# The last quarter of a gate-and-up tile waits unsplit, in a buffer of its own, while the down product runs

## The chip, the core and the metric

The kernel runs on one core of one Trainium2 chip. The metric is the device time of one execution in microseconds (us). Six things work at the same time: TensorE (PE in the profile, with PEld for its weight loads), VectorE (DVE), ScalarE (ACT), GpSimd (POOL), SyncE (SP, which here only issues DMAs) and the DMA engines. Each engine runs its own list of instructions; they wait for each other through semaphores.

## What is computed

One step of a decoder trunk of width 1024, on 512 prompt rows and 8 sample rows (520 columns in all, kept as two halves of 260): a SwiGLU feed-forward block, a mixer (a pooling mixer beside a state-space mixer), a second feed-forward block, a last norm. The change lies in the two feed-forward blocks alone:

```python
FFN_DIM = 2816

def _swiglu(x, wg, wu, wd):
    return (jax.nn.silu(x @ wg) * (x @ wu)) @ wd

h = h + 0.5 * _swiglu(_rms_norm(h, ffn1_norm[l]), ffn1_w_gate[l], ffn1_w_up[l], ffn1_w_down[l])
...
h = h + 0.5 * _swiglu(_rms_norm(h, ffn2_norm[l]), ffn2_w_gate[l], ffn2_w_up[l], ffn2_w_down[l])
```

All data are float32, and the outputs have to be exact to about that.

## The kernel before, in words

**Splitting.** To reach float32 accuracy from a faster matmul type, every weight tile is split into a high part (a ScalarE cast, line 107) and a low part (a VectorE subtraction, line 108), and each product is three matmuls (lines 117 to 119): high by high, high by the low part of the other side, low by high. Each matmul has 260 columns.

**Tiles of the feed-forward block.** The 2816 hidden rows are 22 tiles f of 128. For each f the gate and the up weights are loaded as one raw pair of two 128x1024 halves (lines 250 to 252). A scheme with seven products in place of eight (in the manner of Strassen) forms sums of their quarters (lines 258 to 260) and splits: the whole gate half ("a", line 253, used by products 1 and 2), two tiles of sums ("c" and "d", lines 261 and 262, used by 7 and 5, and by 6 and 3), and the last quarter of the up half ("b", line 263, used by product 4 alone). So `whi_9b` in the profile is the high part of the last quarter of f = 9. Each of the seven products is 12 matmuls (4 blocks j by 3) into one of the PSUM tiles A (products 1, 6, 7, 4) and BE (2, 3, 5).

**Homes.** The split parts "a" and "b" live in two tags, `whi` and `wlo`, with three buffers each of 128x1024 (lines 103 and 253, 263). I call a pair of such buffers a home; there are three. The weights of the down product use the same three homes (line 114). The tiles "c" and "d" have homes of their own (`shi`, `slo`, two each). A home is free again when the last matmul that reads it is done.

**Chunks.** The 22 tiles go in chunks of 8, 8 and 6 (`CHUNKS`). After the tiles of a chunk comes its down product (`down`, line 339): eight units d of 128 output rows, each with 48 matmuls over the chunk's 8 tiles (`part`, line 343), and then two VectorE instructions that add the unit to `h` (`done`, lines 356 and 360). Ahead of the down product, lines 320 to 322 of `rest` already load and split the first tile but one of the next chunk (hi + 1, which is f = 9 and f = 17), make its product 1, and finish tile hi. Its other products are written behind the down product. In the second block each unit d of the first two down products also carries one or two steps of the update of the sample states (line 377), with ScalarE instructions at line 814, VectorE ones at line 816 and DMAs on GpSimd's queue.

**What sets the order.** The program is written in the order above, and a scheduler orders each engine's list when the program is built: it runs a model of the time, and at every moment takes of each engine's instructions the one written first among those that the model holds ready. So a product that is written late can be taken early to fill a gap. A buffer goes to whoever asks first in that order. On the chip each list then runs as it stands.

**Raw buffers.** There are two raw pairs (line 92). The halves of a pair also receive down weights, two units to a pair (`raw_tile`, line 96). A pair is free when the last split or sum that reads it is done; SP then issues the next load.

Of the kernel before, what the change touches and what calls it, by code (L numbers as in the profile page):

```python
# [9 lines left out]
F32 = mybir.dt.float32  # L10
# [6 lines left out]
P = 128  # L17
# [16 lines left out]
CHUNKS = (8, 8, 6)  # L34
# [28 lines left out]
def tile_trunk_step(ctx: ExitStack, tc: tile.TileContext, ins: dict, outs: dict):  # L63
    nc = tc.nc
# [6 lines left out]
    wp = ctx.enter_context(tc.tile_pool(name="wp", bufs=3, side="right"))  # L71
# [19 lines left out]
    def raw_pair(name):  # L91
        return wp.tile([P, 2, 1024], F32, tag="raw", bufs=2, name=f"raw_{name}")
# [9 lines left out]
    def split(src, n, name, hp, nb, tags):  # L102
        hi, lo = (hp.tile([P, 1024], F32R, tag=t, bufs=nb, name=f"{t}_{name}")[:, :n] for t in tags)
        h, l = hi, lo
        if len(src.shape) == 3:
            h, l = (t.rearrange("p (j c) -> p j c", j=src.shape[1]) for t in (hi, lo))
        nc.scalar.copy(h, src)  # L107
        nc.vector.tensor_tensor(out=l, in0=src, in1=h.bitcast(F32), op=ALU.subtract)  # L108
        return hi, lo
# [6 lines left out]
    def mm3(ps, whi, wlo, xhi, xlo, start, stop, **kw):  # L116
        nc.tensor.matmul(ps, whi, xhi, start=start, stop=False, **kw)  # L117
        nc.tensor.matmul(ps, whi, xlo, start=False, stop=False, **kw)  # L118
        nc.tensor.matmul(ps, wlo, xhi, start=False, stop=stop, **kw)  # L119

    def ws(w, k, m=P):
        return w[:, k * m : (k + 1) * m]
# [73 lines left out]
    class Ffn:  # L196
# [4 lines left out]
        def __init__(self, nx, i, wx, gp, direct):  # L201
            self.nx, self.i, self.wx, self.gp, self.direct = nx, i, wx, gp, direct
            self.states = None
            self.w, self.A, self.BE, self.ac, self.g, self.tg, self.raw, self.banks, self.behind = ({} for _ in range(9))

        def plain_load(self, f, j=None):
# [40 lines left out]
        def load(self, f):  # L247
            i, wx, src = self.i, self.wx, ins[f"w{self.i}gu"]
            n = f"{i}_{f}"
            raw = raw_pair(n)  # L250
            nc.sync.dma_start(out=raw[:, 0], in_=src[2 * f])
            nc.sync.dma_start(out=raw[:, 1], in_=src[2 * f + 1])
            d1 = split(raw[:, 0], 1024, f"{n}a", wp, 3, ("whi", "wlo"))
            s1 = wx.tile([P, 2, 512], F32, tag="sw", bufs=2, name=f"s1_{n}")
            s2 = wx.tile([P, 2, 512], F32, tag="sw", bufs=2, name=f"s2_{n}")
            up0 = raw[:, 1, :512].unsqueeze(1).to_broadcast([P, 2, 512])
            diag = bass.AP(up0.tensor, up0.offset - 1024, [up0.ap[0], (1536, 2), up0.ap[2]])
            nc.vector.tensor_tensor(out=s1, in0=diag, in1=up0, op=ALU.add)  # L258
            nc.vector.tensor_tensor(out=s2[:, 0], in0=s1[:, 1], in1=raw[:, 0, :512], op=ALU.add)
            nc.vector.tensor_tensor(out=s2[:, 1], in0=s2[:, 0], in1=raw[:, 0, 512:], op=ALU.add)  # L260
            e1 = split(s1.rearrange("p q c -> p (q c)"), 1024, f"{n}c", wx, 2, ("shi", "slo"))
            e2 = split(s2.rearrange("p q c -> p (q c)"), 1024, f"{n}d", wx, 2, ("shi", "slo"))
            d2 = split(raw[:, 1, 512:], 512, f"{n}b", wp, 3, ("whi", "wlo"))
            self.w[f] = {1: (d1, 0), 2: (d1, 4), 7: (e1, 0), 5: (e1, 4), 6: (e2, 0), 3: (e2, 4), 4: (d2, 0)}

        def product(self, f, p):
            js = range(KD // 2)
            if f not in self.A:
                with tc.issue_after(self.behind[f]) if f in self.behind else nullcontext():
                    self.load(f)  # L270
                n = f"{self.i}_{f}"
                self.A[f] = ps[0].tile([P, 512], F32, tag="A", bufs=2, name=f"A{n}")
                self.BE[f] = ps[0].tile([P, 2, 512], F32, tag="BE", bufs=2, name=f"BE{n}")
                self.ac[f] = [self.wx.tile([P, 2, HB], F32, tag="ac", bufs=3, name=f"ac{n}_{q}") for q in range(2)]
            slot, dst, opens = {1: (0, 0, True), 2: (1, 1, True), 5: (3, 2, True), 6: (5, 0, False),
                                3: (2, 2, False), 7: (4, 0, False), 4: (6, 0, False)}[p]
            out = self.A[f] if dst == 0 else self.BE[f][:, dst - 1]
            (whi, wlo), k0 = self.w[f][p]
            xth, xtl = self.nx[:2]
            for j in js:  # L280
                mm3(out[:, :HB], ws(whi, k0 + j), ws(wlo, k0 + j), xth[:, j, slot], xtl[:, j, slot], opens and j == 0,
                    j == KD // 2 - 1, skip_group_check=True)
            a, c = self.ac[f]
            keep = {1: a[:, 0], 6: a[:, 1], 7: c[:, 0], 5: c[:, 1]}.get(p)
            if keep is not None:
                nc.scalar.copy(keep, out[:, :HB])  # L286
            if p == 7:
                nc.vector.tensor_tensor(out=c[:, 0], in0=c[:, 0], in1=c[:, 1], op=ALU.add)
# [800 lines left out]
```

## Time and profile before

| what | value |
|---|---|
| time of the kernel, median of 3 runs (lowest, highest) | 1012.86 us (1012.05, 1013.91) |
| time of the profiled execution | 1014.71 us |
| its span, first to last instruction | 1012.8 us |
| instructions | 19354 |
| mean granted TensorE clock | 0.993 |
| DVE busy | 807.1 us, 80% of the span |
| ACT busy | 526.1 us, 52% |
| POOL busy | 85.9 us, 8% |
| moved by DMA | 114.44 MB, mean 113 GB/s |

The four places that the change touches, by the time in the profiled execution at which the down product in question runs on PE: first block, first chunk (f = 9 waits) 110.6 to 161.1 us and second chunk (f = 17) 239.1 to 289.9; second block, first chunk 731.5 to 783.6 and second chunk 861.6 to 916.8.

How to read it: a row of the timeline gives start, duration, engine, line, operation, what it writes from what, and in brackets how long the engine sat idle before it and who released it. The duration of a matmul is modelled from issue to drain and overlaps with the next, so lost PE time is read from the distance of starts, not from busy shares alone. In rows by windows, each engine has its busy time and in brackets its number of instructions; PEclk is the granted clock, 1.00 at full speed.

### The profile page before, as it was taken

The page shows a single profiled execution, that of the slowest core. Times are in us where ns is not written, and L with a number is a line of the kernel's source. Part 1 is how long each engine was busy: PE and PEld are TensorE (multiplying, and loading weights), DVE is VectorE, ACT ScalarE, POOL GpSimd, SP SyncE. Part 2 cuts the span into 40 slices and gives each one's busy share as a digit, 9 for nine tenths or more (in the row PEclk, how much of TensorE's full clock was granted, in tenths as well). Part 3 has the DMA queues.
Part 4 walks back from the last instruction along what each step waited for, and adds up shares of the span by engine and source line. Part 5 has one row for each costly group of instructions (what it writes and reads, how often), then busy time and mean ns, then how long its engine had stood idle before and what let it go on. Part 6 is the DMA issues. An engine that isn't in the chain of part 4 may idle for free.

```text
span 1012.8 us, 19354 instructions
## 1 busy us (share of the span) xinstructions
PE 977.1 (96%) x7850; PEld 953.8 (94%) x7850; DVE 807.1 (80%) x1408; ACT 526.1 (52%) x877; POOL 85.9 (8%) x157
## 2 busy tenths in 40 slices
PE   7999999999999999999999999999999999999994
PEld 6999999999999999999899989899999999989994
DVE  7999556995569688788979987999847999467866
ACT  7566324664146455685855235666633666434552
POOL 0000000000000000157311000100013000120000
PEclk9999999999999999999999999999999999999997
DMA  6333222332223233363244421332345423453203
GB/s 193 109 125 126 84 84 94 117 105 97 92 84 105 86 105 111 103 200 116 90 144 125 141 84 43 122 126 87 122 137 184 135 108 111 103 188 123 94 32 84
DMA packets 44072, 114.44 MB, mean 113 GB/s; under 512 B 6408, under 2 KB 15560, under 8 KB 43984
## 3 DMA queue, kind: packets, MB, share of 16 engines
q1 hardware_dynamic: 40912, 103.78, 30.0%
q0 software_dynamic: 3072, 9.44, 3.8%
q8 instruction: 61, 1.00, 0.4%
q14 instruction: 27, 0.22, 0.1%
HBM read 105.86 MB, written 7.34 MB: 112 GB/s over the span
## 4 chain that ended last, share of the span: by engine, by line
PE 84%; DVE 8%; ACT 3%; DMA 2%; issue 1%; POOL 0%; SPq 0%; DVEq 0%; ACTq 0%
PE A L117 8%; PE A L118 7%; PE A L119 7%; PE dn L119 6%; PE dn L117 6%; PE BE L117 6%; PE BE L119 6%; PE dn L118 6%; PE BE L118 6%; PE P L230 2%; PE wo L117 2%; PE wo L118 2%; PE wo L119 2%; PE inz L117 2%; DMA raw<-in_w2gu 2%; PE inz L119 2%
## 5 line engine op out<-in xcount | busy, mean ns | idle before, releaser
L117 PE MATMUL dn<-g,whi_1d 128*128 128x260 f32 x352 | 99.5, 283 | 1.8 <-ACT whi_1d L107 1.6
L356 DVE SCALAR_TENSOR_TENSOR td<-dn,r_f 128x520 f32<-128x520 f32 x40 | 27.8, 698 | 90.8 <-PE dn L119 90.8
L118 PE MATMUL dn<-g,whi_1d 128*128 128x260 f32 x352 | 99.4, 283 | 0.0
L119 PE MATMUL dn<-g,wlo_1d 128*128 128x260 f32 x352 | 99.1, 283 | 0.0
L119 PE MATMUL dn<-g,wlo_2d 128*128 128x260 f32 x256 | 73.6, 288 | 3.7 <-DVE wlo_2d L108 3.7
L117 PE MATMUL dn<-g,whi_2d 128*128 128x260 f32 x256 | 73.1, 286 | 0.4 <-ACT whi_2d L107 0.4
L118 PE MATMUL dn<-g,whi_2d 128*128 128x260 f32 x256 | 73.0, 285 | 0.0
L117 PEld LDWEIGHTS dn<-g,whi_1d 128*128 128x128 f32 x352 | 66.2, 188 | 2.4 <-ACT whi_1d L107 2.0
L118 PEld LDWEIGHTS dn<-g,whi_1d 128*128 128x128 f32 x352 | 66.3, 188 | 0.0
L119 PEld LDWEIGHTS dn<-g,wlo_1d 128*128 128x128 f32 x352 | 66.1, 188 | 0.0
L286 ACT COPY ac<-A 128x260 f32<-128x260 f32 x123 | 45.8, 373 | 35.8 <-PE A L119 34.3
L107 ACT CAST whi_1d<-raw_1d 128x1024 fp32r<-128x1024 f32 (+1 forms) x24 | 23.4, 979 | 70.8 <-PE dn L118 62.3
L258 DVE TENSOR_TENSOR s<-raw 128x1024 f32<-128x1024 f32 x41 | 49.9, 1218 | 7.4 <-DMA raw<-in_w2gu 7.4
L119 PEld LDWEIGHTS dn<-g,wlo_2d 128*128 128x128 f32 x256 | 48.9, 191 | 4.6 <-DVE wlo_2d L108 4.6
L230 PE MATMUL P<-xg_f,raw 128*128 128x260 f32 x192 | 45.3, 393 | 5.8 <-DMA raw<-in_w1gu 5.3
L117 PEld LDWEIGHTS dn<-g,whi_2d 128*128 128x128 f32 x256 | 49.1, 192 | 0.6 <-ACT whi_2d L107 0.6
L118 PEld LDWEIGHTS dn<-g,whi_2d 128*128 128x128 f32 x256 | 49.0, 191 | 0.0
L230 PEld LDWEIGHTS P<-xg_f,raw 128*128 128x128 f32 x192 | 37.0, 196 | 11.7 <-ACT xg_f L179 5.3
L118 PE MATMUL wo<-catg,whi_wo 128*128 128x260 f32 x128 | 36.4, 285 | 1.3 <-DVE catg L946 1.3
L117 PE MATMUL wo<-catg,whi_wo 128*128 128x260 f32 x128 | 37.3, 292 | 0.3 <-DVE h L915 0.3
L117 PE MATMUL inz<-xh_mx,whi_inz 128*128 128x260 f32 x128 | 36.8, 287 | 0.0
L117 PE MATMUL inx<-xh_mx,whi_inx 128*128 128x260 f32 x128 | 36.4, 285 | 0.0
(1339 smaller groups left out, 3918.2 us busy)
## 6 DMA issues: line engine op xcount, KB each, us to landing
raw<-in_w2gu SPq DMA_DIRECT2D x44, 512.0 KB, 4.4
raw<-in_w1gu SPq DMA_DIRECT2D x42, 512.0 KB, 4.4
raw_1d<-in_w1d SPq DMA_DIRECT2D x16, 512.0 KB, 4.4
raw_2d<-in_w2d SPq DMA_DIRECT2D x16, 512.0 KB, 4.7
raw_wo<-in_w_out SPq DMA_DIRECT2D x12, 512.0 KB, 4.5
ab<-scr_acs SPq DMA_DIRECT2D x8, 512.0 KB, 4.6
h<-in_state_ssm SPq DMA_DIRECT2D x16, 256.0 KB, 4.4
raw_inz<-in_w_in SPq DMA_DIRECT2D x8, 512.0 KB, 3.9
```

What stands on the lines that cost most here:

```text
L107: nc.scalar.copy(h, src)
L117: nc.tensor.matmul(ps, whi, xhi, start=start, stop=False, **kw)
L118: nc.tensor.matmul(ps, whi, xlo, start=False, stop=False, **kw)
L119: nc.tensor.matmul(ps, wlo, xhi, start=False, stop=stop, **kw)
L230: nc.tensor.matmul(self.banks[f, u][b][:, :HB], ws(self.raw[f][:, u], j + 4 * q), xg[:, slot[q]], start=j == q == 0, stop=j == 3 and q == ...
L258: nc.vector.tensor_tensor(out=s1, in0=diag, in1=up0, op=ALU.add)
L286: nc.scalar.copy(keep, out[:, :HB])
L356: nc.vector.scalar_tensor_tensor(out=t, in0=banks[d][:, :, :HB], scalar=-0.5, in1=self.nx[3].rearrange("p (b t) -> p b t", b=2), op0=ALU.mult,
```

## The change

For the two tiles f that lie ahead of a down product (9 and 17, in both blocks), the last quarter of the up half is not split when the tile is loaded. ScalarE copies it as it is (128x512 float32) into a buffer of its own, tag `held` in the pool of the gated activations, 2 KB on each partition. The split moves to the first product of that tile other than product 1, which is written behind the down product; it then takes a home of tags `whi` and `wlo` as before. For all other tiles nothing changes. What is computed is the same.

```diff
             self.states = None
+
+            self.held = {CHUNKS[0] + 1: None, CHUNKS[0] + CHUNKS[1] + 1: None}
...
             e2 = split(s2.rearrange("p q c -> p (q c)"), 1024, f"{n}d", wx, 2, ("shi", "slo"))
-            d2 = split(raw[:, 1, 512:], 512, f"{n}b", wp, 3, ("whi", "wlo"))
-            self.w[f] = {1: (d1, 0), 2: (d1, 4), 7: (e1, 0), 5: (e1, 4), 6: (e2, 0), 3: (e2, 4), 4: (d2, 0)}
+            self.w[f] = {1: (d1, 0), 2: (d1, 4), 7: (e1, 0), 5: (e1, 4), 6: (e2, 0), 3: (e2, 4)}
+            if f in self.held:
+                self.held[f] = self.gp.tile([P, 512], F32, tag="held", name=f"held{n}")
+                nc.scalar.copy(self.held[f], raw[:, 1, 512:])
+            else:
+                self.quarter(f, raw[:, 1, 512:])
+
+        def quarter(self, f, src):
+            self.w[f][4] = split(src, 512, f"{self.i}_{f}b", wp, 3, ("whi", "wlo")), 0
...
+            if p != 1 and 4 not in self.w[f]:
+                self.quarter(f, self.held[f])
```

## The prediction

> **What bounds the kernel now.** I read the page first, then PE by windows, then the timeline of PE, ACT and DVE at the four places.
>
> ```profile
> PE 977.1 (96%) x7850; PEld 953.8 (94%) x7850; DVE 807.1 (80%) x1408; ACT 526.1 (52%) x877; POOL 85.9 (8%) x157
> PE 84%; DVE 8%; ACT 3%; DMA 2%; issue 1%; POOL 0%; SPq 0%; DVEq 0%; ACTq 0%
> ```
>
> PE is busy for 96% of the span and holds 84% of the chain that ended last. Only time in which PE stands still, inside those few per cent, can be won. By windows, first a long stretch of feed-forward tiles, then 18 us around the start of each of the four down products:
>
> ```profile
> 160.00:235.00 75.00, 75.00 (x627) 75.00 (x626) 69.03 (x96) 45.67 (x73) 0.00 (x0) 1.00 0.29 99
> 104.00:122.00 18.00, 16.91 (x137) 16.28 (x136) 10.75 (x14) 7.43 (x12) 0.00 (x0) 1.00 0.17 59
> 233.00:251.00 18.00, 16.90 (x136) 16.28 (x135) 10.65 (x14) 7.27 (x11) 0.00 (x0) 1.00 0.21 63
> 726.00:744.00 18.00, 16.52 (x134) 15.89 (x133) 10.57 (x18) 9.44 (x22) 1.39 (x3) 1.00 0.26 75
> 856.00:874.00 18.00, 16.53 (x134) 15.90 (x133) 10.56 (x18) 9.44 (x21) 1.26 (x3) 1.00 0.26 76
> ```
>
> In the long stretch PE never stops; 75 us for 627 matmuls are 0.12 us each. DVE is 92% busy there, so it is close behind. In the four short windows PE is idle for 1.09, 1.10, 1.48 and 1.47 us, 5.14 in all. Why, at the first place, ACT shows:
>
> ```profile
> 104.54 0.63 ACT L107 CAST whi_9b<-raw 128x512 fp32r<-128x512 f32 x1 [0.39 <-PE BE L118]
> 109.22 1.05 ACT L107 CAST whi_1d<-raw_1d 128x1024 fp32r<-128x1024 f32 x1 [0.77 <-PE A L118]
> 118.33 1.05 ACT L107 CAST whi_1d<-raw_1d 128x1024 fp32r<-128x1024 f32 x1 [5.00 <-PE dn L118]
> 119.78 1.04 ACT L107 CAST whi_1d<-raw_1d 128x1024 fp32r<-128x1024 f32 x1 [0.39 <-PE A L118]
> 126.80 1.05 ACT L107 CAST whi_1d<-raw_1d 128x1024 fp32r<-128x1024 f32 x1 [5.98 <-PE dn L118]
> ```
>
> At 104.54 the home that 8a left goes to 9b. Unit 0 of the down product gets 8b's, at 109.22. Unit 1 has none: 9a and 9b lie in two, unit 0 in the third. Its split waits 5 us, until unit 0's matmuls are done. Then the scheduler takes product 4 of tile 9 as a filler, which frees 9b's home for unit 2 (119.78). From there two homes alternate and each split is a whole unit early. So 9b blocks a home just for the first unit, and the price is paid at the start of each down product. On PE it looks like this, first block, then second:
>
> ```profile
> 110.70 0.28 PE L118 MATMUL dn<-g,whi_1d 128*128 128x260 f32 x1
> 111.22 0.39 PE L117 MATMUL A<-xth_f,shi_9c 128*128 128x260 f32 x1 [0.23 <-ACT ac L286]
> 118.25 0.29 PE L117 MATMUL A<-xth_f,whi_9b 128*128 128x260 f32 x1
> 119.82 0.28 PE L118 MATMUL dn<-g,whi_1d 128*128 128x260 f32 x1
> 120.88 0.39 PE L117 MATMUL dn<-g,whi_1d 128*128 128x260 f32 x1 [0.77 <-ACT whi_1d L107]
> ...
> 731.59 0.28 PE L118 MATMUL dn<-g,whi_2d 128*128 128x260 f32 x1
> 732.48 0.39 PE L119 MATMUL dn<-g,wlo_2d 128*128 128x260 f32 x1 [0.61 <-DVE wlo_2d L108]
> 739.68 0.28 PE L118 MATMUL dn<-g,whi_2d 128*128 128x260 f32 x1
> 740.74 0.39 PE L117 MATMUL A<-xth_f,whi_9b 128*128 128x260 f32 x1 [0.78 <-ACT ac L286]
> ```
>
> PE starts unit 0 with two matmuls on the high part, has no low part yet, goes off to tile 9, and does the same again at unit 1. ACT and DVE are named as releasers, but what they lacked was a home.
>
> **The change part by part.** *Removed:* the two stalls at each place. Lost time is the distance of starts beyond 0.12 us. First block: 111.22 - 110.70 - 0.12 = 0.40, and 120.88 - 119.82 - 0.12 = 0.94, together 1.34. Second block: 732.48 - 731.59 - 0.12 = 0.77, and 740.74 - 739.68 - 0.12 = 0.94, together 1.71. The windows of the second chunks have the same idle time to 0.01 us, so I take the same there: 2 x 1.34 + 2 x 1.71 = 6.1 us.
>
> Do they go? With 9b out of the way unit 0 takes 8a's home at 104.54. The cast lasts 1.05 (to 105.6), the low part 1.22 in the place that 9b's had:
>
> ```profile
> 105.94 0.68 DVE L108 TENSOR_TENSOR wlo_9b<-raw,whi_9b 128x512 fp32r<-128x512 f32 x1
> 109.02 0.29 PE L119 MATMUL A<-xth_f,wlo_8b 128*128 128x260 f32 x1
> 126.92 0.70 DVE L356 SCALAR_TENSOR_TENSOR td<-dn,r_f 128x520 f32<-128x520 f32 x1 [4.76 <-PE dn L119]
> 128.27 1.22 DVE L108 TENSOR_TENSOR wlo_1d<-raw_1d,whi_1d 128x1024 fp32r<-128x1024 f32 x1
> 763.00 1.22 DVE L108 TENSOR_TENSOR wlo_2d<-raw_2d,whi_2d 128x1024 fp32r<-128x1024 f32 x1
> 106.65 23.67 SPq L113 DMA_DIRECT2D raw_1d<-in_w1d  x6
> ```
>
> 105.94 + 1.22 is 107.2, and PE is through with 8b at 109.1: 2 us early. Unit 1 takes 8b's home at 109.2 and is split by about 111.5; PE wants it after 48 matmuls, at 109.1 + 5.8 = 114.9, 3.4 us later. Unit 2 comes when unit 0 is done, which is the state that the trace already shows: cast at 126.80, low part done at 129.5, 2.7 us of the 5.8 that a unit lasts. In the second block the state updates stand between; the tightest, with two steps, ends at 764.2 for a release near 759.5, still 1 us early. So no new stall takes the place of the old.
>
> *Kept:* a short gap of 0.26 us ahead of product 4 of tile 8, behind a ScalarE copy that the change does not touch.
>
> ```profile
> 107.22 0.28 PE L119 MATMUL A<-xth_f,wlo_9a 128*128 128x260 f32 x1
> 107.60 0.39 PE L117 MATMUL A<-xth_f,whi_8b 128*128 128x260 f32 x1
> ```
>
> It checks the sum: a busy PE is shown 0.16 us past the next start (0.28 - 0.12), so three gaps at four places add 12 x 0.16 = 1.9 to the 5.14 idle; less the four kept, 1.0, this gives 6.0. The scheduler may now fill it with matmuls of unit 0; that would be up to 1.0 more.
>
> *Added:* four ScalarE copies of 128x512. None is in the trace; the 128x512 cast takes 0.63, the 128x1024 one 1.05, so 0.6 within 0.4 to 1.05. It takes the ACT slot of 9b's cast, needs no home and so no wait. Nothing on PE reads it before the end of the down product. I cost it at nothing, with ACT 52% busy as cover; bare it would be 2.5 us over four places.
>
> *Moved:* four casts (0.63) and four subtractions (0.68) from the dense stretch ahead of the down product to its end, and 12 matmuls of product 4 with them; products 6 and 7, which were fillers, probably too. PE's total stays. Raw pair 9 is let go by a copy that need not wait, not by 9b's low part at 106.6, so the SP issue at 106.65 moves up by up to 2 us: no loss.
>
> At the end of the down product the quarter needs a home:
>
> ```profile
> 155.27 1.05 ACT L107 CAST whi_10a<-raw 128x1024 fp32r<-128x1024 f32 x1 [4.69 <-PE dn L118]
> 156.74 1.22 DVE L108 TENSOR_TENSOR wlo_10a<-raw,whi_10a 128x1024 fp32r<-128x1024 f32 x1
> 161.01 0.62 ACT L107 CAST whi_10b<-raw 128x512 fp32r<-128x512 f32 x1 [4.69 <-PE dn L118]
> 145.00:160.00 15.00, 15.00 (x128) 15.00 (x127) 9.06 (x11) 2.10 (x2) 0.00 (x0) 1.00 0.20 71
> ```
>
> Before, the home that unit 6 left went to 10a (155.27) and that of unit 7 to 10b (161.01). Now 9b takes the first, 10a the second, 10b waits for 9a. 10a is then ready about 1.05 + 1.22 + two VectorE adds of 0.7 = 3.7 us after the end of the down product. But PE has more to do there too: products 5, 6, 3, 7, 2 and 4 of tile 9, six of 1.45 us or 8.7 us, where before three were left. I cost this at nothing; the cover is 5 us, and DVE has room, 60% busy. Uncovered it is the last rival below.
>
> *Not settled:* the last unit of the down products of the second block stalls before, too.
>
> ```profile
> 777.80 0.39 PE L119 MATMUL dn<-g,wlo_2d 128*128 128x260 f32 x1 [0.73 <-DVE wlo_2d L108]
> 903.52 1.22 DVE L258 TENSOR_TENSOR s<-raw 128x1024 f32<-128x1024 f32 x1 [4.52 <-DMA raw<-in_w2gu]
> 907.48 0.28 PE L118 MATMUL dn<-g,whi_2d 128*128 128x260 f32 x1
> 909.52 0.45 PE L119 MATMUL dn<-g,wlo_2d 128*128 128x260 f32 x1 [1.77 <-DVE wlo_2d L108]
> 913.02 0.33 PE L117 MATMUL dn<-g,whi_2d 128*128 128x260 f32 x1
> 910.00:920.00 10.00, 10.00 (x73) 10.00 (x73) 5.60 (x11) 2.19 (x4) 0.54 (x1) 0.84 0.49 165
> ```
>
> DVE's list has a sum for the next tile ahead of unit 7's low part, and that sum waits for a DMA. It costs 0.73 + 0.16 = 0.9 us in the first chunk. In the second it costs 909.52 - 907.48 - 0.12 = 1.9, a smaller gap of 0.6 before it (0.41 shown idle for the cast, + 0.16), and then a clock of about half from 909.52 to 913.02: 16 matmuls in 3.5 us, against 1.9, so 1.6. Together 4.1. What decides it is when the raw pair lands among the state DMAs. Both the release of that pair and the last unit move up together with the shorter start, so I take no change. The ends: all of it gone, -5.0; or the first chunk as bad as the second, +3.2.
>
> The Trainium skill ("TensorE: Matmul & The Clock Gate", section "What's actually happening") says that TensorE falls to half its clock after an idle window of about 3.4 us and needs as long to come back. The rows agree on the half clock and on its 3.5 us, but here an idle time of only 1.9 with 0.6 before it was enough. By that rule the stalls at the starts, each under 1 us, carry no clock term, and the sum stays as it is; the same gate is what makes a longer stall at the end dear.
>
> *Sum:* -6.1 + 0 + 0 + 0. For the profiled execution that is 1014.71 - 6.1 = 1008.6; it lies 1.85 above the median of the runs, and against the median of 1012.86 the forecast is 1006.8.
>
> **The rivals.**
>
> *The ends get better too.* If the next tile's pair arrives in time in the second chunk, the 4.1 us go: 1012.86 - 6.1 - 4.1 = 1002.7. For it: it is a race of a DMA, worse by 3 us in one chunk than in the other with the same program. Against: nothing in the change speeds up those DMAs.
>
> *The home is taken again.* The copy is ready long before a down unit needs a home. If the scheduler's model holds a unit's raw tile as not landed when a home falls free, the quarter takes it, and all is as before but for a hidden copy: 1012.9. Against: units are written ahead of the quarter and so go first, and SP's issue at 106.65 for units 2 to 7 leaves 8 us to unit 2's turn at 114.9. For: the same greedy choice took product 4 as a filler at 118.25.
>
> *The end of the down product becomes the stall; slower.* The quarter sits in the third home, 10a begins only behind unit 7, and PE runs out of tile 9. This decides if the scheduler still takes 9's products 6, 7 and others as fillers early, so that fewer than three (3.7 us at 1.45) are left behind unit 7. PE then waits up to 3.7, and falls to half the clock for 1.6: 5.3 at each of four places, 21.2 - 6.1 = +15.1, or 1028; where one of the fillers remains (1.45 less), about 1022. Against: what made the fillers necessary is gone.
>
> **How the numbers follow.** Forecast 0.52; better ends 0.18; home taken again 0.14; slower 0.16. The measurement can tell 0.2% from no change, 2.0 us. Forecast and better ends are faster by more: 0.70. Home taken again is within: 0.14. Slower: 0.16. The forecast's own range is 1004.8 (the kept gaps filled and a part of the end stalls) to 1010.0 (first chunk's end +3.2). For 8 in 10 the range goes down to the better ends, 1002.5, and up over the middle of no change, 1013.2; it leaves out the slower case and a few per cent on either side.
>
> **What would show it.** Right: in the changed profile the first cast of down weights stands where 9b's was, about 4.5 us before PE reaches unit 0, the second waits for product 4 of tile 8 (A, line 118) and not for a down matmul; PE goes from 8b through units 0 and 1 with no break; the four windows at the starts keep about 0.1 us of idle time; the 128x512 casts of 9b and 17b stand near the end of the down product and wait for one of its matmuls; behind unit 7 PE does not wait for a home. Wrong: 9b's cast early again with a filler of product 4 behind unit 0 (home taken again), or PE waiting for `whi_10a` or `wlo_10a` (slower). If the sum is right but the time is off by 1 to 5 us, the end of the second block's down products, with its clock, is where to look.

## The result, and the profile after

The kernel with the change takes 1002.59 us (median of 5 runs, 1000.94 to 1003.79) against 1012.86 (5 runs, 1011.94 to 1013.91): a ratio of 0.9903, 95% interval 0.9890 to 0.9916, so 8.5 to 11.1 us faster. Forecast was 1006.8 in a range of 1002.5 to 1013.2. The way is right and the time lies in the range, at its lower end: the gain of 10.3 is two thirds larger than the 6.1 of the sum. It is outside the forecast's own range (1004.8 to 1010.0), and inside the whole range, whose lower bound came from the rival of the better ends, by only 0.1 us.

The profiled execution of the changed kernel took 1003.51 us with a span of 1000.5, 12.3 shorter than before. Line numbers behind line 204 moved by two to eleven: the sums of line 258 are now at 260, the down product's adds of 356 and 360 at 367 and 371. PE by windows of 18 us around the start of each of the four down products (span of the window; then busy time and number of instructions of PE, PEld, DVE, ACT, POOL; granted clock, DMA share, GB/s):

```profile
106.00:124.00 18.00, 18.00 (x153) 18.00 (x152) 10.52 (x15) 6.29 (x9) 0.00 (x0) 1.00 0.24 89
232.00:250.00 18.00, 18.00 (x152) 18.00 (x152) 10.49 (x15) 6.79 (x10) 0.00 (x0) 1.00 0.29 108
722.00:740.00 18.00, 18.00 (x152) 18.00 (x152) 11.56 (x19) 10.33 (x22) 1.61 (x3) 1.00 0.43 139
849.00:867.00 18.00, 18.00 (x152) 18.00 (x152) 11.58 (x19) 10.22 (x22) 1.60 (x3) 1.00 0.39 130
```

The 5.14 us of idle time of these windows are gone to the last hundredth, and 152 or 153 matmuls stand where 134 to 137 stood. ACT's part of the timeline at the first place shows why, and it is the pattern that was forecast:

```profile
104.76 1.06 ACT L107 CAST whi_1d<-raw_1d 128x1024 fp32r<-128x1024 f32 x1 [0.39 <-PE BE L118]
111.62 1.05 ACT L107 CAST whi_1d<-raw_1d 128x1024 fp32r<-128x1024 f32 x1 [2.95 <-PE A L118]
114.84 1.05 ACT L107 CAST whi_1d<-raw_1d 128x1024 fp32r<-128x1024 f32 x1 [1.64 <-PE dn L118]
...
150.72 0.62 ACT L107 CAST whi_9b<-held 128x512 fp32r<-128x512 f32 x1 [4.69 <-PE dn L118]
156.46 1.05 ACT L107 CAST whi_10a<-raw 128x1024 fp32r<-128x1024 f32 x1 [5.12 <-PE dn L118]
```

Unit 0's cast stands where 9b's was, unit 1 waits for product 4 of tile 8 (A), only unit 2 for a down matmul. The quarter takes the home that unit 6 leaves, and 10a that of unit 7. PE, at the place where the kept gap of 0.26 us had been:

```profile
107.44 0.28 PE L119 MATMUL A<-xth_f,wlo_9a 128*128 128x260 f32 x1
107.56 0.28 PE L117 MATMUL dn<-g,whi_1d 128*128 128x260 f32 x1
...
109.97 0.28 PE L119 MATMUL dn<-g,wlo_1d 128*128 128x260 f32 x1
110.09 0.29 PE L117 MATMUL A<-xth_f,whi_8b 128*128 128x260 f32 x1
```

The scheduler had unit 0 ready so early that it set 21 of its matmuls ahead of product 4 of tile 8, so PE reaches unit 0 2.8 us behind the start of its cast, where the forecast had 4.5. The copies, four in all, cost 0.62 us each and run long before anyone needs them, the first 13 us ahead of the slot of 9b's cast in which the forecast had it (rows of all instructions on the new buffer, min/median/max in ns, first and last start):

```profile
L268 ACT COPY held<-raw x4: 620/622/625, 91.6 to 835.5; 128x512 f32<-128x512 f32 x4
```

To see where the time went, I took the distance on PE from the first matmul of tile 9 to the first of tile 13, which holds a whole down product, and so for the other three places (17 to 21 in the first block, 17 to 20 in the second). The work of PE in between is the same in all kernels here (720 matmuls, 636 in the last column). In us:

| kernel | block 1, 9 to 13 | block 1, 17 to 21 | block 2, 9 to 13 | block 2, 17 to 20 |
|---|---|---|---|---|
| before | 88.17 | 88.44 | 89.82 | 82.88 |
| changed | 86.31 | 86.56 | 86.48 | 76.37 |
| difference | -1.86 | -1.88 | -3.34 | -6.51 |

That is 13.6 us; 1.3 come back elsewhere, mostly ahead of tile 9 (0.2) and in the last stretch (1.2). The profiled executions lie above the medians of their kernels, by 1.9 us before and 0.9 after, so this pair of profiles overstates the gain by about 1 us. In the first block the starts are all there is. In the second the ends add to it. The end of the last of these down products, VectorE's timeline of the changed kernel, beside the rows of before at 903.52 and 909.52:

```profile
889.10 1.23 DVE L260 TENSOR_TENSOR s<-raw 128x1024 f32<-128x1024 f32 x1 [1.85 <-DMA raw<-in_w2gu]
894.09 1.22 DVE L108 TENSOR_TENSOR wlo_2d<-raw_2d,whi_2d 128x1024 fp32r<-128x1024 f32 x1
896.13 0.70 DVE L367 SCALAR_TENSOR_TENSOR td<-dn,r_f 128x520 f32<-128x520 f32 x1 [0.83 <-PE dn L119]
```

Unit 7's low part ends at 895.3, and PE comes to it only after 896 (the 896.13 row waits for unit 6's last matmul). No stall, no half clock.

### The profile page after: what moved, and what is told of

It is laid out like the page before. It is cut to its first block, busy times and chain, and to the rows that moved or that the text cites. A ratio compares the mean times of both kernels' runs of the same rounds, so it can differ in the third digit from the quotient of the medians.

```text
span 1000.5 us, 19362 instructions
## 1 busy us (share of the span) xinstructions
PE 971.7 (97%) x7850; PEld 951.4 (95%) x7850; DVE 806.9 (81%) x1408; ACT 528.7 (53%) x881; POOL 87.8 (9%) x157
## 4 chain that ended last, share of the span: by engine, by line
PE 88%; DVE 6%; ACT 2%; POOL 2%; issue 1%; DMA 0%; SPq 0%; DVEq 0%; ACTq 0%
PE A L119 8%; PE A L117 8%; PE A L118 8%; PE dn L117 7%; PE dn L119 7%; PE dn L118 7%; PE BE L117 6%; PE BE L119 6%; PE BE L118 6%; PE P L232 4%; PE wo L117 2%; PE wo L118 2%; PE wo L119 2%; PE inz L117 2%; PE inz L119 2%; PE inz L118 2%
```

## The experiments

My theory for the starts: the third home. Its rivals: that the quarter's split was put off, which lightens VectorE and ScalarE ahead of the down product; that the copy lets go of the raw pair earlier; and that the gain has little to do with the starts. For the ends: VectorE's low part of unit 7 stands behind a sum that waits for a DMA; rivals: ScalarE's wait for a state row, and chance.

**The change in one block alone.**

```diff
-            self.held = {CHUNKS[0] + 1: None, CHUNKS[0] + CHUNKS[1] + 1: None}
+            self.held = {CHUNKS[0] + 1: None, CHUNKS[0] + CHUNKS[1] + 1: None} if i == 1 else {}
```

> The quarter is held unsplit in the first block alone. Home theory (the third home is blocked for the first unit of each down product, and every gap also costs its second matmul 0.1 us): PE time from the first matmul of tile 9 to that of tile 13 falls from 88.17 to 86.3 us, from 17 to 21 from 88.44 to 86.6; the second block stays at 89.82 (9 to 13) and, but for the race of a DMA, 82.88 (17 to 20). Total -3.7 us. Rival (most of the gain sits at the ends of the second block's down products and comes with any change of the program): second block shorter too, total more than 6 us faster.

Measured: 86.31 and 86.56 in the first block, as in the changed kernel to 0.01 us; 89.46 and 82.21 in the second. Ratio 0.9968 (0.9954 to 0.9982), -3.2 us. The first block's gain is its own. The second block is 0.4 and 0.7 us shorter than before without being changed: its starts have the same stalls, but at the ends the gap of 0.9 was 0.6, and the smaller gap ahead of the half clock was absent.

With `i == 2` instead:

> The quarter is held unsplit in the second block alone. Home theory: first block as before (88.17 and 88.44), second block 86.5 (9 to 13) and 76.4 (17 to 20), of which 2.3 us each are from the start of the down product; total -9.8 us in the trace. Rival (the ends vary by chance from one execution to the next): second block between 84.5 and 90, without order.

Measured: 88.18 and 88.47, as before; 86.48 and 77.50 in the second block. Ratio 0.9926 (0.9908 to 0.9945), -7.5 us (5.6 to 9.3), less than the 9.8 expected from the one pair of profiles. The places are as the home theory has them but for the last figure, 1.1 us longer than in the changed kernel, and PE's timeline at that end shows it:

```profile
900.85 0.28 PE L118 MATMUL dn<-g,whi_2d 128*128 128x260 f32 x1
902.00 0.39 PE L119 MATMUL dn<-g,wlo_2d 128*128 128x260 f32 x1 [0.87 <-DVE wlo_2d L108]
902.22 0.28 PE L117 MATMUL dn<-g,whi_2d 128*128 128x260 f32 x1
902.34 0.28 PE L118 MATMUL dn<-g,whi_2d 128*128 128x260 f32 x1
```

The stall is still possible there, 902.00 - 900.85 - 0.12 = 1.03 us of it. The next row shows another thing: after a stall the second matmul starts 0.22 after the first, the third 0.12 again. Each stall costs 0.1 more than its gap.

**A home of its own, split at once.** First block alone; the quarter is split at load time as before, into two small buffers.

```diff
+                qhi, qlo = (self.gp.tile([P, 512], F32R, tag=t, name=f"{t}_{n}b") for t in ("qhi", "qlo"))
+                nc.scalar.copy(qhi, raw[:, 1, 512:])
+                nc.vector.tensor_tensor(out=qlo, in0=raw[:, 1, 512:], in1=qhi.bitcast(F32), op=ALU.subtract)
+                self.w[f][4] = (qhi, qlo), 0
```

> First block alone: the quarter is split when the tile is loaded, as before, but into two small buffers of its own, so no split is put off and no copy is added. Home theory: same as with the quarter held in the first block, 86.3 and 86.6 us, total -3.7. Rival (what helps is the lighter ScalarE and VectorE load ahead of the down product, and the work kept for its end): 88.2 and 88.4 as before, total within 1 us.

Measured: 86.46 and 86.73, ratio 0.9957 (0.9940 to 0.9974). Unit 0's cast again stands where 9b's was, and PE's idle time at the start is gone:

```profile
105.27 1.05 ACT L107 CAST whi_1d<-raw_1d 128x1024 fp32r<-128x1024 f32 x1 [0.38 <-PE BE L118]
105.00:123.00 18.00, 18.00 (x151) 17.93 (x151) 11.75 (x16) 7.07 (x9) 0.00 (x0) 1.00 0.36 118
```

Of 1.86 us, 1.71 come from the home alone. Of the rest, 0.15, PE's rows show 0.12 at product 4 of tile 8, which starts at 108.33 behind only two matmuls of unit 0 (108.19), with its second matmul at 108.55. It was tried in the first block alone, since it takes 4 KB on each partition in place of the 2 KB of the held copy.

**The copy without the home.** Both blocks; the quarter is split from its copy at once, into the usual home.

```diff
                 nc.scalar.copy(self.held[f], raw[:, 1, 512:])
+                self.quarter(f, self.held[f])
```

> The quarter is copied into its spare buffer, but split from it at once, into the usual home, in both blocks. Home theory: the stalls at the starts are all back, 88.2, 88.4 in the first block and about 89.8, 82.9 in the second, total within 2 us of before; the four copies cost nothing. Rival (the gain is the earlier release of the raw pair, which the copy gives): near the changed kernel, -6 us or more.

Measured: 88.17, 88.43, 89.21, 82.46; ratio 0.9992 (0.9977 to 1.0006). The first window, moved by 0.2 us:

```profile
104.20:122.20 18.00, 16.91 (x137) 16.28 (x136) 10.78 (x14) 7.41 (x12) 0.00 (x0) 1.00 0.16 58
```

16.91 and 137, as before the change. The stalls at the starts are back to the hundredth, in the second block too (0.26, 0.77 and 0.94), the copies cost nothing that shows, and the earlier release of the raw pair gains nothing at the starts. The 0.6 and 0.4 us by which the second block is shorter than before lie at its ends.

**The sums of the next tile behind unit 7.** Kernel before; in the second block VectorE's part of the next tile's load is queued behind the low part of the down product's last unit (`low` is the last subtraction of `split`; the lines that keep it are left out here):

```diff
                     units[d] = load_unit(...)
+                    if d == KD - 1 and after is None and self.i == 2:
+                        self.behind[hi + 2] = low[0].ins
```

> Kernel before, but in the second block VectorE's sums of the next tile are queued behind the low part of the down product's last unit. Theory of the ends (that low part stands in VectorE's list behind a sum that waits for the raw pair's DMA): the stalls at units 7 go, 9 to 13 from 89.82 to 88.7, 17 to 20 from 82.88 to 78.6, with no half clock; total about -5. Rival (the stall is ScalarE's, which waits for the DMA of a state row ahead of the high part): the gaps stay, total within 1 us.

Measured: 90.52 and 80.33; ratio 0.9976 (0.9957 to 0.9994), -2.4 us. A miss: the second chunk got 2.5 us shorter and lost its half clock, but the first got 0.7 longer, and gaps of 0.5 and 0.9 stayed at unit 7 in both. The theory named one wait, the rival another, and both are there. ScalarE's timeline at the second end:

```profile
902.01 1.28 ACT L817 ACTIVATE so<-br,sxdt 128x128 f32<-128x128 f32 x4 [4.72 <-DMA br<-scr_bc]
905.89 1.28 ACT L817 ACTIVATE so<-br,sxdt 128x128 f32<-128x128 f32 x4 [2.59 <-DMA br<-scr_bc]
907.08 1.03 ACT L108 CAST whi_2d<-raw_2d 128x1024 fp32r<-128x1024 f32 x1
```

Unit 7's high part stands behind two state steps that wait for their rows; with VectorE free, this wait is the one that is late.

> Changed kernel with the same order at the ends. Theory of the ends: nothing is left to win, 86.5 and 76.4 us as in the changed kernel, time 1002.6 within 1 us. If in some executions of the changed kernel the sum still comes late, it is up to 1 us faster and spreads less. Rival (the later sums delay the tiles behind): slower by 1 to 3 us.

The same order in the changed kernel: 86.48 and 76.37, 1002.92 us (1002.27 to 1003.44), ratio 0.9886 (0.9853 to 0.9919). As expected, these runs show nothing left to win there.

**Both lists in order.** On top of the last edit, kernel before, the state steps of units 6 and 7 are written behind the units' splits:

```diff
-                for _ in range(STATES[d] if self.states is not None else 0):
-                    next(self.states)
+                if d < KD - 2:
+                    for _ in range(STATES[d] if self.states is not None else 0):
+                        next(self.states)
                 part(d, range(n))
+                if d >= KD - 2:
+                    for _ in range(STATES[d] if self.states is not None else 0):
+                        next(self.states)
```

> Kernel before with both lists put in order at the ends of the second block: VectorE's sums of the next tile behind the low part of unit 7, and the state steps of units 6 and 7 written behind these units' splits, so that ScalarE's wait for a state row no longer stands ahead of unit 7's high part. Theory (two waits for DMAs in line, one on each engine): no stall at unit 7, 9 to 13 about 88.4 and 17 to 20 about 78.3, as without the state updates; total -6. Rival (another wait, for the home or for a state buffer, comes next): 0.5 us or more left at each end.

Measured: 89.74 and 79.39; ratio 0.9986 (0.9973 to 1.0000), -1.4 us where -6 was expected. A miss again, and the rival's case, with gaps of 0.8 and 0.7 left at unit 7: a third wait, on VectorE, whose timeline has

```profile
774.37 1.14 DVE L823 SCALAR_TENSOR_TENSOR hs<-hs,sdec,so 128x128 f32<-128x128 f32 x4 [5.12 <-ACT whi_2d L108]
775.42 0.70 DVE L359 SCALAR_TENSOR_TENSOR td<-dn,r_f 128x520 f32<-128x520 f32 x1
776.15 0.70 DVE L363 TENSOR_TENSOR h<-td,h 128x520 f32<-128x520 f32 x1
776.77 1.22 DVE L109 TENSOR_TENSOR wlo_2d<-raw_2d,whi_2d 128x1024 fp32r<-128x1024 f32 x1
```

a state step ahead of unit 7's low part. (The view names ScalarE's cast, which was done at 773.5, and the ScalarE step that this one reads was done at 772.6. What came last was most likely the state itself, whose load GpSimd's queue had issued at 767.29.) So read, the states' DMAs are late, and each order only chooses which instruction waits for them.

**Without the states.** The update of the sample states is left out (one output is not computed), in the kernel before and in the changed one.

```diff
-    f2["ffn"].states = f2["states"](f2["st"])
-    next(f2["ffn"].states)
```

> Kernel before without the update of the sample states (nss is not computed). Theory: without their DMAs and their ScalarE and VectorE work the ends have no stall; the starts keep theirs. 9 to 13 about 88.5 us and 17 to 20 about 78.2, close to the first block's pattern. Rival (the ends stall for the home too): 89.8 and 82.9.

> Changed kernel without the update of the sample states (nss is not computed). Home theory: each of the four places gains 1.9 to 2.3 us against the kernel before without it, so 7.5 to 8.3 us in all; the rest of what the change gave was at the ends. Rival: 10 us or more between the two.

Measured before: 88.17, 88.44, 88.42, 78.30. Changed: 86.32, 86.56, 86.60, 76.37. The four differences are 1.85, 1.88, 1.82 and 1.93, 7.5 us in all, and the medians, 1010.43 and 1003.23 us, lie 7.2 apart. Without the states the starts are the whole gain, and the second block behaves as the first. With them, the profiled execution of the changed kernel is no slower at these places than without: what the states had cost PE there is gone in that execution, though not in every one, as shown below.

**The ends as a race.** In the changed kernel the scheduler puts 8 matmuls of product 7 between the issue of the next tile's raw load and unit 7, as PE's timeline shows between 883.67 and 884.64, with the load issued at 882.95:

```profile
882.95 0.43 SPq L254 DMA_DIRECT2D raw<-in_w2gu  x1
883.67 0.28 PE L118 MATMUL A<-xtl_f,shi_17c 128*128 128x260 f32 x1
884.64 0.28 PE L119 MATMUL dn<-g,wlo_2d 128*128 128x260 f32 x1
```

The 8 matmuls last 8 x 0.12 = 0.96 us. I made them go behind the down product (`self.last[f]` is the down product's last matmul; the lines that set it are left out here):

```diff
-                self.product(f, p)
+                with tc.issue_after(self.last[f]) if f in self.last else nullcontext():
+                    self.product(f, p)
```

> Changed kernel, but TensorE takes no product of tile 9 or 17 (other than 1 and 4) before the last matmul of the down product, so the 8 matmuls of product 7 that now stand between the raw pair's load and unit 7 (0.96 us) go behind it. Lead theory (those 8 matmuls give the load 13.0 us to unit 7 in place of 12.0): starts without stalls as in the changed kernel (86.3 and 86.6 in the first block), but unit 7 waits again in the second block, 87.0 to 87.6 (9 to 13) and 78.5 to 80.5 (17 to 20). Rival (in the changed kernel the load landed early by chance or for another reason): 86.5 and 76.4.

Measured: 86.29 and 86.57; in the second block 87.18 and 76.59. The first chunk stalls again, as the lead theory says:

```profile
767.09 0.28 PE L118 MATMUL dn<-g,whi_2d 128*128 128x260 f32 x1
767.79 0.39 PE L119 MATMUL dn<-g,wlo_2d 128*128 128x260 f32 x1 [0.42 <-DVE wlo_2d L108]
```

The second stalled by 0.1 alone, against the expectation: its load landed early this time. Ratio 0.9901 (0.9881 to 0.9921), 1003.17 us against 1003.85 with the 8 matmuls (the next run, made beside it): in the kernel's time their loss can't be seen.

> The changed kernel once more. Home theory and the ends as a race: 86.3, 86.6 and, in the second block, 86.5 again, 17 to 20 either 76.4 (load in time) or up to 77.5 (as in the run with the second block alone). Rival (the ends are gone for good): 76.4 again. Ratio to the kernel before 0.990.

Measured: 86.32, 86.56, 86.48 and 77.47; 1003.85 us (1003.36 to 1004.41, 5 runs), ratio 0.9909 (0.9891 to 0.9927). The last figure is the late case. The same kernel, another execution, and PE's timeline has the stall:

```profile
896.45 0.28 PE L118 MATMUL dn<-g,whi_2d 128*128 128x260 f32 x1
897.55 0.39 PE L119 MATMUL dn<-g,wlo_2d 128*128 128x260 f32 x1 [0.82 <-DVE wlo_2d L108]
```

Put together, with all times counted from the issue of the second half of the raw load (rows such as 882.95 or 894.69 on SP's queue): when the sum starts that waits for it, when unit 7's low part is done, and when PE would need it (start of the third matmul of unit 7 less the stalls there). The run with a home of its own has the second block as before.

| kernel, chunk of block 2 | sum starts | low part done | needed | stall |
|---|---|---|---|---|
| before, first | 7.2 | 13.1 | 12.3 | 0.9 |
| before, second | 8.8 | 14.8 | 12.3 | 2.5 and half clock |
| block 1 alone, first | 6.9 | 12.8 | 12.3 | 0.6 |
| block 1 alone, second | 8.2 | 14.1 | 12.3 | 1.9 and half clock |
| home of its own, first | 6.2 | 12.2 | 12.3 | none |
| home of its own, second | 8.2 | 14.2 | 12.3 | 1.9 and half clock |
| changed, first | 6.4 | 12.6 | 13.2 | none |
| changed, second | 6.2 | 12.4 | 13.2 | none |
| changed once more, second | 8.0 | 14.2 | 13.2 | 1.0 |
| block 2 alone, second | 8.0 | 14.2 | 13.2 | 1.0 |
| changed, product 7 behind, first | 6.9 | 12.8 | 12.3 | 0.6 |
| changed, product 7 behind, second | 6.4 | 12.3 | 12.2 | 0.1 |

The stall is the low part's time less the need, wherever that is above zero, to 0.1 us. The low part comes 6 us behind the sum, with VectorE's list full in between. The change moved the need from 12.3 to 13.2, by the 8 matmuls; taking them away moved it back. The other half is when the load lands, and that varies without the change as well: at the first end of a second block as before, the sum started after 7.2, 6.9 and 6.2 us, and the last of these left no stall. With the need at 13.2 none of the three would stall, so at the first end the 8 matmuls would be enough by themselves. At the second end they are not: low parts at 14.1 to 14.8, as in the block as before, would still leave 0.9 to 1.6 us. That this end had no stall at all in the first profile of the changed kernel took an early load (6.2) besides, and what made it early is not shown.

## Why the prediction was right, point by point

*The stalls at the starts go, because of the home:* right, and shown. The home alone gives 1.71 of 1.86 us; copy and release without it give nothing.

*Their size, 1.34 and 1.71 us, 6.1 in all:* mis-sized. Without the states the four starts measured 7.5 us; with them the second block's are larger, about 2.3 each by its rows, 8.3 in all. Two terms lacked. The sum kept the gap of 0.26 ahead of product 4 of tile 8 at each place and gave its filling as a chance; it was filled at all four, 1.0 us. And it took only the gap of a stall, where the next matmul distance is also 0.1 longer: three gaps in the first block make 0.3, and 0.26 + 1.34 + 0.3 = 1.90 against 1.86 measured; in the second 0.26 + 1.71 + 0.3 = 2.27. The cross-check by idle time, which came to 6.0, has the same hole, since such a matmul is drawn 0.39 long and counts as busy.

*The copy at nothing:* right; 0.62 us each, at 91.6 us for a use at 150.7. *The moved split and product 4 at nothing:* right; PE is busy for all of 104 to 176 us in the changed kernel, and its waits are empty there and over both down products of the second block. The rival in which the end becomes the stall did not come; tile 9 kept four or five products for it.

*"I take no change" at the ends:* the step that failed. The reason given for it, that the raw pair's release and the last unit move up together, overlooked that the scheduler's fillers are free to move: 8 of their matmuls came to lie between the two. In the first chunk this took the whole 0.9 away, about -1.1 with the matmul after it; the load was 0.8 us faster too, which alone would nearly have done it. In the second, -4.2 in the profiled execution, of which about 1 us came back where the load was late. The bound of -5.0 for all of it was too narrow by 0.3, again by the slow matmul after each gap. The rival of the better ends was given for "a race of a DMA", with nothing in the change to help it. The race is there, and the change did help, by the 0.9 us of the need; the rest was the load's time of landing. That the measured time fell inside the range at all was luck to that extent. By the medians the ends are worth less than by the one pair of profiles: 7.2 us without the states are the starts', and with the states the change gave 10.3, and 9.2 by the later ratio of 0.9909, which leaves an estimated 2 to 3 us for the ends in place of 5.3.

*The half clock:* as read. With a gap of 1.9 us the second end dropped to half the clock in the kernel before and in the three others whose second block stalls as before's; with 1.0 it did not, in two executions. So where the load is late, the 0.96 us of the 8 matmuls are worth more than themselves there. By windows, the kernel with the first block alone, and the changed one once more (granted clock third from the end):

```profile
905.00:911.00 6.00, 5.91 (x36) 5.91 (x37) 3.53 (x8) 0.00 (x0) 0.54 (x1) 0.72 0.80 262
```

```profile
896.40:903.00 6.60, 5.78 (x48) 5.57 (x47) 3.96 (x8) 0.62 (x1) 1.08 (x2) 1.00 0.68 238
```

The first runs 36 matmuls in 6.0 us behind its gap, the second, gap included, 48 in 6.6.

*What stays open:* why the load lands after 6.2 us in one execution and after 8.0 in the next. In all four profiles of the second end with the block as before, or with the copy but not the home, it took 8.2 to 8.8, in the changed block 6.2, 8.0 and 8.0. Without the states the sum started after 5.3 us at all four ends, in both kernels, so the states make it late; what makes it vary with them was not tried. (Those two kernels do not settle the stalls at the ends by this alone, since there 17 more matmuls stand between the load and unit 7 than in the kernel before.)

## What to carry to other kernels

Count buffers at the moment where one phase hands over to the next: something that lies split and ready for a later phase can block the one buffer that the present one needs for its second step, and a small raw copy frees it at nearly no cost. When a stall is priced, take the distance from the last good start to the second good start, not the gap alone. And where a stall ends on a race with a DMA, ask what the scheduler may now put between issue and use; changing only the order of the waiting lists moved that stall to the next wait, twice.

## What was not expected of the hardware

After a stall of TensorE the second matmul starts 0.22 us behind the first (902.00 to 902.22), the next again 0.12. The Trainium skill ("TensorE: Matmul & The Clock Gate", section "What's actually happening") gives an idle window of about 3.4 us before the clock halves; here a single gap of 1.9 us was enough in three kernels (in the kernel before with one of 0.6 just ahead of it), and gaps of 1.0 were not in two executions, so for this kernel the measured 1.9 us counts.
